# Expert queries in one float32 product instead of three products of parts, and VectorE in GpSimd's place for the residues beside the routing

## The chip, the cores and the metric

The kernel runs on one core of one Trainium2 chip. The metric is the device time of one execution in microseconds (us); the time of a kernel is the median of several executions. The profiler recorded one execution of it, and every row below comes from that record. TensorE is called PE in the rows (PEld its weight loads), VectorE DVE, ScalarE ACT, GpSimd POOL, SyncE SP. Everything is float32 at the level of the model, 256 tokens of width 1024, with 16 more "meta" tokens in the second block.

## The reference, cut to what matters

A first block (two layers of feed-forward, mixed attention, feed-forward) is followed by a second block of two layers. Each of these two layers ends in a "PEER" stage, an expert layer with 16384 experts, and it is the start of that stage that the change touches:

```
def peer(x, wq, subkey1, subkey2, u, v):        # x: normed rows
    q = x @ wq                                  # 8 heads, 2 halves of 128
    s1, s2 = q[half 0] . subkey1, q[half 1] . subkey2    # 128 scores each
    t1, i1 = top_k(s1, 16);  t2, i2 = top_k(s2, 16)
    t, at = top_k(t1[:, None] + t2[None, :], 16)         # 16 experts of a head
    gate = softmax(t)
    # all experts' gelu(x . u_e) * gate_e, summed over v_e
```

In other words: queries, scores, top 16 of each half, the top 16 of their sums, and a softmax over those. That is called the routing here. Beside it the kernel computes gelu(x . u) for all experts densely, and multiplies by the gates afterwards.

## The kernel before, in words

Activations lie transposed: 128 features on the partitions, tokens along the free axis (272 columns in the first PEER stage, 256 in the second, where the meta tokens are dropped).

**Products in three parts.** Most linear layers don't multiply float32 by float32. `weights` (L384) loads a piece of 128x1024 numbers into a tile `w`, and splits each half of it into `wh`, a copy of type float32r made by ScalarE (L398), and `wl`, the residue w - wh (L400), made by VectorE or GpSimd as the letter string `self.lo` says, one letter for each half in turn. Activations are split the same way (`xh`, `xl`, by `split` at L411). `mm3` (L419) then issues three products into one PSUM bank: wh.xh (L422), wh.xl (L423), wl.xh (L424). `w` has a ring of 4 pieces, `wh` and `wl` one of 6 halves each. A few smaller products multiply float32 directly, among them the taps of the conformer's convolution (L1242, 128x128 by 128x272).

**The order of the work** comes from a scheduler that lays the whole program out engine by engine before it runs; each engine then works through its own list strictly in order, and waits where an operand isn't there.

**The rows for the queries.** While the layer before a PEER stage writes its results to `h`, `fresh` (L1175) is called per 128 features; it calls `gained` (L1188), which multiplies h by the norm's gain and splits the product into two tiles of the pair "rr" (ScalarE L1191, VectorE L1192). The division by the root mean square is left for later, since top-k doesn't mind a positive factor.

**The routing** (`route`, L1568): for each of 8 heads, for each half: the weights of the half (L1641), 8 chunks of 128 by `linear` (24 products), a copy of the query (L1645), and two products with the sub-keys (L1649, float32) for two groups of 128 tokens. After both halves `best` (L1591) copies the scores (L1593, ScalarE) and runs VectorE's top-16: MAX (L1562, L1565), index search (L1563, L1566), replacement (L1564), sums (L1600). The 16 meta tokens of all heads go through one more such round at the end. Then `finish` (L1605 to L1635) turns positions into expert numbers and computes the softmax, and `turn` (L1661) transposes the result with three products a group (L1664). Five such groups of L1664 stand on TensorE's list in the first stage (the fifth waits for small DMAs of the meta tokens), four in the second. `keys` (L1483) then casts the result.

**The norm** (`norm`, L1471), called after head 0: the root mean square, eight normed rows (L1475), split into `xh` and `xl`; the residues went to VectorE and GpSimd in turn (`lo="vg"[c % 2]`).

**The experts' first products** (`act`, L1460): for one of 128 groups of 128 experts, one piece of `u`, 24 products with xh and xl, a Gelu. They need nothing of the routing, so that the scheduler lays them beside it. `peer` (L1449) sets `self.lo = "g"` ahead of the routing and for the first 26 of them (PEER_FROM), so that the residues of 16 query pieces and 26 pieces of u, two each, are GpSimd's; from group 26 on it is PEER_LO = 'gv', the two in turn.

Of the kernel before, what the change touches and what calls it, by code (L numbers as in the profile page):

```python
# [17 lines left out]
AF = mybir.ActivationFunctionType  # L18
# [6 lines left out]
T2 = T + NM  # L25
DC = 8
# [3 lines left out]
PIECE, RAW = 1024, 4  # L30
# [155 lines left out]
def _layout1(I):  # L186
# [25 lines left out]
WD = 11  # L212
# [10 lines left out]
W_AN, W_B1, W_DW, W_DB, W_CG, W_CB, W_B2, W_KVN, W_BN, W_FN, W_FIN, W_SUB, W_LAM, NVEC2 = np.cumsum(  # L223
    [0, 8, 16, 8 * CONVW, 8, 8, 8, 8, 8, 8, 16, 8, 1, 4]).tolist()
# [60 lines left out]
class Rows:  # L285
# [6 lines left out]
    z = None  # L292
# [54 lines left out]
class Kernel:  # L347
# [774 lines left out]
    def _second_block(self, ctx, h, out, dump):  # L1122
        nc, I = self.nc, self.I
        self.h = h
        self.rp = self.pool("room", 1, ctx=ctx)
        self.pk = self.pool("pk2", 2, ctx=ctx)
        self.act = self.pool("act2", 1, ctx=ctx)
        nc.scalar.dma_start(h[:, :, 0:NM], I['metaT'])

        def show(n):  # L1130
            if n in dump:
                nc.sync.dma_start(dump[n], h)

        self.following(W_AN, 0, self.pair("xh", "xl"))
        for d in range(DC):
            self.fresh(d, nc.vector if LN_S[d] == 'v' else nc.gpsimd)
        z, s2 = self.z, self.s2
        self.following(W_FN, 0, self.pair("rr"))
        self.conformer(z, s2)
        show('conv')  # L1140
        z, s2 = self.z, self.s2
        self.following(W_KVN, 0, None)
        self.peer(0, 0, z, s2)
        show('peer0')
        z, s2 = self.z, self.s2
        self.following(W_FN + DC, NM, None)
        self.attention(z, s2)
        show('attn')
        z, s2 = self.z, self.s2
        self.following(None, NM, None)  # L1150
        self.peer(1, NM, z, s2)
        r = self.rms_factor(self.s2, NM)[1]
        for c in range(DC):
            nc.vector.scalar_tensor_tensor(h[:, c, NM:], h[:, c, NM:], self.v2(W_FIN + c), r, op0=ALU.mult, op1=ALU.mult)
            if c % 2:
                nc.sync.dma_start(out[:, c - 1:c + 1], h[:, c - 1:c + 1, NM:])
# [5 lines left out]
    def pair(self, *tags):  # L1162
# [3 lines left out]
            return rr[:, 0], rr[:, 1]  # L1166
        return [self.tl(self.act, [128, DC, T2], n, F32R) for n in tags]

    def following(self, gain, t0, parts):

        self.gain, self.t0, self.to = gain, t0, parts
        self.s2 = self.tl(self.act, [128, T2], "ss2", bufs=2)
        self.z = []
# [13 lines left out]

    def gained(self, d, t0, gain, to):  # L1188
        nc, h, g = self.nc, self.h[:, d, t0:], self.v2(gain + d)
        zh, zl = [p[:, d, :T2 - t0] for p in to]  # L1190
        nc.scalar.activation(zh, h, AF.Copy, scale=g)  # L1191
        nc.vector.scalar_tensor_tensor(zl, h, g, zh, op0=ALU.mult, op1=ALU.subtract)  # L1192
        return zh, zl
# [117 lines left out]
    def attention(self, zk, ss):  # L1311
        nc, h, I, C = self.nc, self.h, self.I, self.C2
        mm = nc.tensor.matmul
# [3 lines left out]
        to = self.pair("rr")  # L1317
# [120 lines left out]
                    steps[s](i - lag, n)  # L1438
        self.lo = "v"
        yh, yl = self.pair("xh", "xl")  # L1440
        self.to = self.pair("rr")
        ys = []
        for c in range(DC):
            ys.append((yh[:, c, :T], yl[:, c, :T]))
# [4 lines left out]
    def peer(self, l, t0, z, ss):  # L1449
        nc, h, I = self.nc, self.h, self.I  # L1450
        mm = nc.tensor.matmul
        w = T2 - t0
# [11 lines left out]


        at[0] = ROOM - ROUTE
        self.lo = "g"
        xh, xl = self.pair("xh", "xl")
        x = []

        def norm():  # L1471
            r, ps = self.rms_factor(ss, t0)
            for c in range(DC):
                t = self.tl(self.act, [128, T2], "nrm", bufs=2)[:, :w]
                nc.vector.scalar_tensor_tensor(t, h[:, c, t0:], self.v2(W_FN + DC * l + c), ps, op0=ALU.mult, op1=ALU.mult)  # L1475
                x.append((xh[:, c, :w], xl[:, c, :w]))
                self.split(*x[c], t, lo="vg"[c % 2])
            return r

        self.route(take, ring, l, t0, z, norm, ix)  # L1480
        rr = self.pair("rr")

# [61 lines left out]
        g = 0  # L1544
# [23 lines left out]
    def route(self, take, ring, l, t0, z, norm, ix):  # L1568


        nc, I = self.nc, self.I
        mm = nc.tensor.matmul
        w = T2 - t0
# [17 lines left out]
        def best(r, hd, ps):  # L1591
            s = new_s()
            nc.scalar.activation(s, ps, AF.Copy)  # L1593
            for i in range(2):
                self.top16(r.v[i][:, hd], r.i[i][:, hd], s[:, i])


            c = new_c()
            for o, a, b, n in ((0, 0, 4, 16), (64, 4, 16, 4)):
                nc.vector.tensor_tensor(c[:, o:o + (b - a) * n].rearrange("p (a b) -> p a b", b=n),  # L1600
                                        r.v[0][:, hd, a:b][:, :, None].to_broadcast([128, b - a, n]),
                                        r.v[1][:, hd, 0:n][:, None, :].to_broadcast([128, b - a, n]), op=ALU.add)
            self.top16(r.tv[:, hd], r.tp[:, hd], c)
# [34 lines left out]
        for hd in range(8):  # L1638
            ps = [self.bank("C", 256).rearrange("p (a b) -> p a b", a=2) for _ in chunks]
            for half in range(2):  # L1640
                wq = self.weights(I['f_wq'][l, 2 * hd + half], DC)  # L1641
                pq = self.bank("AD"[half], w)
                self.linear(pq, wq, z)
                q = new_q()
                nc.scalar.activation(q[:, :w], pq, AF.Copy)  # L1645
                if meta:
                    nc.gpsimd.tensor_copy(qm[:, half, hd], q[:, 0:NM])
                for i, c in enumerate(chunks):
                    mm(ps[i][:, half], q[:, c:c + 128], sk[:, half], start=True, stop=True)  # L1649
            if hd == 0:  # L1650
                r = norm()
            for i in range(2):
                best(R[i], hd, ps[i])
# [17 lines left out]
        if meta:  # L1671
            o = take(3, 1, 16)
            finish(M, r[:, 2:3], o)
            t = take(3, 8, 16)
# [40 lines left out]
```

## Time and profile before

| what | value |
|---|---|
| median of 3 executions | 3320.82 us (3313.59 to 3323.24) |
| profiled execution | 3313.82 us, span of its record 3312.0 us |
| first PEER stage: first product with the sub-keys, last L1664 | 1338.5 us, 1478.6 us |
| second PEER stage: the same two | 2430.4 us, 2553.2 us |
| TensorE busy, granted clock in the two stretches | 118.94 of 140.10 us at 0.93; 103.27 of 122.90 us at 0.92 |

The record has 2 us less than the execution that it comes from, and that execution is 7.0 us shorter than the median. Busy time of TensorE counts the pipelined ends of its products, and is longer at a lower granted clock. A window's row gives, for each engine, the busy time in the stretch and the number of instructions.

### The profile page before, as it was taken

The page shows a single profiled execution, that of the slowest core. Times are in us where ns is not written, and L with a number is a line of the kernel's source. Part 1 is how long each engine was busy: PE and PEld are TensorE (multiplying, and loading weights), DVE is VectorE, ACT ScalarE, POOL GpSimd, SP SyncE. Part 2 cuts the span into 40 slices and gives each one's busy share as a digit, 9 for nine tenths or more (in the row PEclk, how much of TensorE's full clock was granted, in tenths as well). Part 3 has the DMA queues.
Part 4 walks back from the last instruction along what each step waited for, and adds up shares of the span by engine and source line. Part 5 has one row for each costly group of instructions (what it writes and reads, how often), then busy time and mean ns, then how long its engine had stood idle before and what let it go on. Part 6 is the DMA issues. An engine that isn't in the chain of part 4 may idle for free.

```text
span 3312.0 us, 69651 instructions
## 1 busy us (share of the span) xinstructions
PE 3182.8 (96%) x27035; PEld 3058.0 (92%) x27035; DVE 2335.8 (71%) x5464; ACT 1663.4 (50%) x3401; POOL 1006.8 (30%) x819
## 2 busy tenths in 40 slices
PE   8999999999999999989999999999998999999998
PEld 8997899999789988889999999999888999999898
DVE  5675676767667578982987549857689397755975
ACT  5564465656546543445444553455354545455454
POOL 0011000001100000764444443444367444444443
PEclk9998899999979999989999999999898999999999
DMA  7652256665215653435444554454244545455454
GB/s 234 188 165 77 75 171 183 185 185 161 80 58 167 184 165 120 134 128 172 148 160 147 165 173 128 157 177 146 89 143 133 185 154 173 153 181 170 135 184 142
DMA packets 140862, 503.14 MB, mean 152 GB/s; under 512 B 17329, under 2 KB 19633, under 8 KB 139889
## 3 DMA queue, kind: packets, MB, share of 16 engines
q1 hardware_dynamic: 137104, 496.06, 47.6%
q8 instruction: 212, 3.47, 0.4%
q10 hardware_dynamic: 3328, 2.36, 0.2%
q14 instruction: 122, 0.99, 0.1%
q0 software_dynamic: 96, 0.26, 0.0%
HBM read 496.36 MB, written 1.05 MB: 150 GB/s over the span
## 4 chain that ended last, share of the span: by engine, by line
PE 75%; DVE 18%; issue 5%; ACT 2%; POOL 0%; DMA 0%; ACTq 0%; SPq 0%; POOLq 0%; DVEq 0%
PE A L422 10%; PE A L423 10%; PE A L424 10%; PE D L422 9%; PE D L423 9%; PE D L424 9%; PE C L422 3%; PE C L423 3%; PE C L424 3%; DVE two L1494 2%; DVE A L1499 2%; DVE wl L400 2%; PE B L758 2%; PE C L1503 1%; DVE room L1600 1%
## 5 line engine op out<-in xcount | busy, mean ns | idle before, releaser
L398 ACT ACTIVATE wh<-w 128x512 fp32r<-128x512 f32 x1856 | 1153.5, 626 | 1284.7 <-PE A L423 507.7
L400 DVE TENSOR_TENSOR wl<-w,wh 128x512 fp32r<-128x512 f32 (+1 forms) x1212 | 859.9, 713 | 550.0 <-ACT wh L398 524.4
L400 POOL TENSOR_TENSOR wl<-w,wh 128x512 fp32r<-128x512 f32 x644 | 888.3, 1385 | 978.1 <-ACT wh L398 938.5
L422 PE MATMUL A<-xh,wh 128*128 128x256 f32 (+2 forms) x1912 | 555.9, 292 | 19.8 <-ACT wh L398 8.4
L423 PE MATMUL A<-xl,wh 128*128 128x256 f32 (+2 forms) x1912 | 554.1, 290 | 3.0 <-DVE xl L330 2.6
L424 PE MATMUL A<-xh,wl 128*128 128x256 f32 (+2 forms) x1912 | 552.3, 289 | 1.3 <-POOL wl L400 1.1
L422 PE MATMUL D<-xh,wh 128*128 128x256 f32 (+2 forms) x1664 | 485.0, 291 | 2.8 <-ACT xh L329 1.5
L423 PE MATMUL D<-xl,wh 128*128 128x256 f32 (+2 forms) x1664 | 480.7, 289 | 3.7 <-DVE xl L330 3.6
L424 PE MATMUL D<-xh,wl 128*128 128x256 f32 (+2 forms) x1664 | 480.1, 289 | 3.8 <-POOL wl L400 3.3
L422 PEld LDWEIGHTS A<-xh,wh 128*128 128x128 f32 x1912 | 368.2, 193 | 24.4 <-ACT wh L398 10.9
L423 PEld LDWEIGHTS A<-xl,wh 128*128 128x128 f32 x1912 | 369.9, 194 | 6.8 <-DVE xl L330 4.9
L424 PEld LDWEIGHTS A<-xh,wl 128*128 128x128 f32 x1912 | 369.8, 193 | 2.8 <-POOL wl L400 1.3
L423 PE MATMUL A<-rr,wh 128*128 128x272 f32 (+1 forms) x1152 | 330.7, 287 | 2.4 <-DVE rr L1192 2.4
L422 PE MATMUL A<-rr,wh 128*128 128x272 f32 (+1 forms) x1152 | 331.2, 288 | 0.8 <-ACT rr L1191 0.8
L424 PE MATMUL A<-rr,wl 128*128 128x272 f32 (+1 forms) x1152 | 329.9, 286 | 0.8 <-POOL wl L400 0.8
L422 PE MATMUL D<-rr,wh 128*128 128x272 f32 (+1 forms) x1152 | 330.3, 287 | 0.0
L424 PE MATMUL D<-rr,wl 128*128 128x272 f32 (+1 forms) x1152 | 329.3, 286 | 0.0
L423 PE MATMUL D<-rr,wh 128*128 128x272 f32 (+1 forms) x1152 | 328.8, 285 | 0.0
L423 PEld LDWEIGHTS D<-xl,wh 128*128 128x128 f32 x1664 | 320.7, 193 | 6.0 <-DVE xl L330 5.8
L422 PEld LDWEIGHTS D<-xh,wh 128*128 128x128 f32 x1664 | 320.3, 192 | 5.8 <-ACT xh L329 3.1
L424 PEld LDWEIGHTS D<-xh,wl 128*128 128x128 f32 x1664 | 320.6, 193 | 5.4 <-POOL wl L400 4.0
L423 PEld LDWEIGHTS A<-rr,wh 128*128 128x128 f32 x1152 | 217.7, 189 | 3.4 <-DVE rr L1192 3.4
(474 smaller groups left out, 6586.7 us busy)
## 6 DMA issues: line engine op xcount, KB each, us to landing
w<-in_u_dram SPq DMA_DIRECT2D x256, 512.0 KB, 3.5
w<-in_v_dram SPq DMA_DIRECT2D x256, 512.0 KB, 3.7
w<-in_ffn_w_dram SPq DMA_DIRECT2D x240, 512.0 KB, 4.4
w<-in_win_f_dram SPq DMA_DIRECT2D x32, 512.0 KB, 3.7
w<-in_f_wq_dram SPq DMA_DIRECT2D x32, 512.0 KB, 3.6
w<-in_ffn_w_dram SPq DMA_DIRECT2D x32, 384.0 KB, 3.1
w<-in_pw_dram SPq DMA_DIRECT2D x24, 512.0 KB, 4.2
w<-in_w_out_dram SPq DMA_DIRECT2D x16, 512.0 KB, 3.8
```

The source lines that it names most:

```text
L398: nc.scalar.activation(h, s, AF.Copy)
L400: (nc.vector if eng == "v" else nc.gpsimd).tensor_tensor(l, s, h, op=ALU.subtract)
L422: mm(ps, wh, xh, start=start, stop=False)
L423: mm(ps, wh, xl, start=False, stop=False)
L424: mm(ps, wl, xh, start=False, stop=stop)
L758: mm(s[:, a:b], q[:, qc * 128:qc * 128 + 128], k[:, :b - a], start=i == 0, stop=False)
L1494: nc.vector.tensor_tensor(two, self.key[:, None].to_broadcast([128, 4, 128, 2]), row(1, 128), op=ALU.is_equal)
L1499: nc.vector.tensor_tensor(A[:, i], one, row(2 + i, n), op=ALU.mult)
L1503: mm(ps[:, k], two[:, k // 2, :, k % 2], A[:, i, k // 2, :, k % 2], start=i == 0, stop=i == 1)
L1600: nc.vector.tensor_tensor(c[:, o:o + (b - a) * n].rearrange("p (a b) -> p a b", b=n), r.v[0][:, hd, a:b][:, :, None].to_broadcast([128, b ...
```

## The change

The queries' products become single float32 products of the raw piece and the raw rows. The tile pair "rr" gives way to one tile of the same bytes (`whole`), `gained` writes the gained rows once, and the route loads each weight piece and multiplies it as it is. Two letters change: `self.lo` ahead of the routing from "g" to "v", which now concerns the 26 pieces of u, and the norm's residues all go to VectorE.

```
@@ second block, and attention's end
-        self.following(W_FN, 0, self.pair("rr"))
+        self.following(W_FN, 0, self.whole())
...
-        self.to = self.pair("rr")
+        self.to = self.whole()
@@
+    def whole(self):
+        return [self.tl(self.act, [128, 2, WD, T2], "rr")[:, 0]]
@@ gained
+        if len(to) == 1:
+            z = to[0][:, d, :T2 - t0]
+            nc.scalar.activation(z, h, AF.Copy, scale=g)
+            return z
         zh, zl = [p[:, d, :T2 - t0] for p in to]
@@ peer
-        self.lo = "g"
+        self.lo = "v"
...
-                self.split(*x[c], t, lo="vg"[c % 2])
+                self.split(*x[c], t)
@@ route
-                wq = self.weights(I['f_wq'][l, 2 * hd + half], DC)
+                wq = self.tl(self.ring, [128, PIECE], "w", bufs=RAW)
+                nc.sync.dma_start(wq, I['f_wq'][l, 2 * hd + half])
                 pq = self.bank("AD"[half], w)
-                self.linear(pq, wq, z)
+                for c in range(DC):
+                    mm(pq, wq[:, c * 128:c * 128 + 128], z[c], start=c == 0, stop=c == DC - 1)
```

The scheduler lays the two PEER starts out anew; on VectorE, ScalarE, GpSimd and SyncE the lists elsewhere are the same. Three places show it. Names end in a number of the tile; line numbers after the change are up to 10 higher (L1649 is L1659, L1624 is L1632, L1626 is L1634, L1627 is L1635).

TensorE in the first routing, a stretch of one head's queries (A and D are PSUM banks of the two halves, C the scores), before:

```order
L1649 MATMUL C_15932<-room_15926 128x128
L1649 MATMUL C_15933<-room_15926 128x128
L422 MATMUL A_16106<-rr_14625,wh_16102 128x272
L423 MATMUL A_16106<-rr_14625,wh_16102 128x272
L424 MATMUL A_16106<-rr_14625,wl_16103 128x272
L422 MATMUL A_16106<-rr_14625,wh_16102 128x272
```

And the same place of a head after:

```order
L1653 MATMUL A_16246<-rr_14625,w_16244 128x272 x5
L1653 MATMUL D_16261<-rr_14625,w_16259 128x272
L1659 MATMUL C_16174<-room_15918 128x128
L1659 MATMUL C_16175<-room_15918 128x128
L1653 MATMUL D_16261<-rr_14625,w_16259 128x272 x7
L1653 MATMUL A_16314<-rr_14625,w_16312 128x272 x3
```

Three entries a chunk have become one, and the products with the sub-keys stand between fewer of them.

GpSimd at the start of the first routing (xl and nrm are the norm's, wl residues of query weights, room_ the queries' meta columns), before:

```order
L1647 COPY room_15926<-room_15926 128x16
L400 TENSOR_TENSOR wl_16331<-w_16328,wh_16330 128x512
L400 TENSOR_TENSOR wl_16335<-w_16328,wh_16334 128x512
L1647 COPY room_15926<-room_15926 128x16
L417 TENSOR_TENSOR xl_15930<-nrm_16030,xh_15929 128x272
L400 TENSOR_TENSOR wl_16370<-w_16367,wh_16369 128x512
```

And after, from the load of the sub-keys to the first residue that GpSimd still has:

```order
L1584 DMA room_15918<-in_sk_dram 128x256
L1657 COPY room_15918<-room_15918 128x16 x2
L435 TENSOR_TENSOR ny_15964<-rv_15962,half_69 128x3
L1657 COPY room_15918<-room_15918 128x16 x14
L400 TENSOR_TENSOR wl_17576<-w_17573,wh_17575 128x512
```

Between the copies nothing is left on GpSimd; its next residue belongs to group 26 of u.

VectorE in the last third of the first routing (`finish`), before:

```order
L1624 TENSOR_TENSOR room_15926<-room_15926,iota_1460_8073 128x1024 x2
L1635 TENSOR_TENSOR room_15926<-room_15926 128x16
L1626 TENSOR_TENSOR room_15926<-room_15926 128x1024
L1617 SCALAR_TENSOR_TENSOR room_15926<-room_15926 128x16
L1626 TENSOR_TENSOR room_15926<-room_15926 128x1024
L1627 TENSOR_REDUCE room_15926<-room_15926 128x64
```

And after:

```order
L1632 TENSOR_TENSOR room_15918<-room_15918,iota_1460_8073 128x1024
L400 TENSOR_TENSOR wl_17466<-w_17463,wh_17465 128x512
L400 TENSOR_TENSOR wl_17470<-w_17463,wh_17469 128x512
L1632 TENSOR_TENSOR room_15918<-room_15918,iota_1460_8073 128x1024
L400 TENSOR_TENSOR wl_17502<-w_17499,wh_17501 128x512
L1634 TENSOR_TENSOR room_15918<-room_15918 128x1024
```

Residues of u stand between the steps of `finish`: 57 of them from the first MAX to the cast in `keys` in the first stage, 55 in the second, where there were none. On TensorE the last group of L1664 stood in the 20th group of u and stands in the 29th.

## Rows read from the trace of the kernel before

**Rows 1.** Page, part 1: busy us (share of the span) and instructions.

```profile
PE 3182.8 (96%) x27035; PEld 3058.0 (92%) x27035; DVE 2335.8 (71%) x5464; ACT 1663.4 (50%) x3401; POOL 1006.8 (30%) x819
```

**Rows 2.** Windows: stretch, length, PE, PEld, DVE, ACT, POOL busy (x), clock, DMA share, GB/s.

```profile
1338.50:1478.60 140.10, 118.94 (x873) 115.55 (x872) 130.38 (x526) 65.32 (x135) 96.71 (x89) 0.93 0.38 119
1478.60:1520.00 41.40, 41.40 (x329) 41.40 (x330) 17.25 (x21) 20.90 (x41) 22.50 (x17) 1.00 0.59 198
...
2430.30:2553.20 122.90, 103.27 (x809) 101.50 (x809) 117.02 (x480) 57.25 (x122) 88.41 (x68) 0.92 0.42 135
2553.20:2600.00 46.80, 46.80 (x398) 46.80 (x398) 23.76 (x22) 25.67 (x50) 30.66 (x23) 1.00 0.59 185
```

**Rows 3.** TensorE's waits, both routings: us, times, longest; last row before the second.

```profile
PE C L1664 <- DVE room L1620: 6.6, 1, 6.6
PE C L1649 <- ACT room L1593: 6.1, 4, 2.0
...
PE C L1664 <- DVE room L1620: 10.5, 1, 10.5
...
PE A L423 <- DVE rr L1192: 2.4, 5, 0.8
```

**Rows 4.** Timeline of DVE and POOL, first routing: start, length, engine, line, operation.

```profile
1345.32 0.20 DVE L1600 TENSOR_TENSOR room<-room 128x48 f32<-128x48 f32 x1
...
1345.70 1.08 DVE L1600 TENSOR_TENSOR room<-room 128x64 f32<-128x64 f32 x1
...
1345.40 1.29 POOL L400 TENSOR_TENSOR wl<-w,wh 128x512 fp32r<-128x512 f32 x1 [0.47 <-ACT wh L398]
```

**Rows 5.** DVE by form, first routing: busy us, mean ns; then 1417.5 to 1423.9.

```profile
L1600 DVE TENSOR_TENSOR room<-room 128x64 f32<-128x64 f32 x17 | 9.5, 559 | 0.0
...
L1626 DVE TENSOR_TENSOR room<-room 128x1024 f16<-128x1024 f16 x8 | 9.5, 1201 | 0.0
...
L1600 DVE TENSOR_TENSOR room<-room 128x48 f32<-128x48 f32 x17 | 9.3, 545 | 0.0
...
L417 DVE TENSOR_TENSOR xl<-nrm,xh 128x272 fp32r<-128x272 f32 x4 | 4.1, 1025 | 0.0
...
L1614 DVE SCALAR_TENSOR_TENSOR room<-room 128x128 f32<-128x128 f32 x2 | 1.6, 812 | 0.0
...
L1600 DVE TENSOR_TENSOR room<-room 128x64 f32<-128x64 f32 x2 | 0.4, 200 | 0.0
...
L1614 DVE SCALAR_TENSOR_TENSOR room<-room 128x128 f32<-128x128 f32 x1 | 0.3, 279 | 0.0
```

**Rows 6.** DVE by form, second routing.

```profile
L1624 DVE TENSOR_TENSOR room<-room,iota 128x1024 f16<-128x1024 f16 x8 | 12.7, 1626 | 0.0
...
L1600 DVE TENSOR_TENSOR room<-room 128x64 f32<-128x64 f32 x16 | 7.7, 480 | 0.0
```

**Rows 7.** Timeline of DVE ahead of the routing; POOL's residues by form, first routing.

```profile
1309.93 1.90 DVE L400 TENSOR_TENSOR wl<-w,wh 128x512 fp32r<-128x512 f32 x3 [0.16 <-ACT wh L398]
...
L400 POOL TENSOR_TENSOR wl<-w,wh 128x512 fp32r<-128x512 f32 x68 | 91.7, 1366 | 45.6 <-ACT wh L398 45.4
```

**Rows 8.** TensorE: L1242 (ns min/median/max); timeline of taps, products with 272, 256 columns.

```profile
L1242 PE MATMUL B<-room x232: 390/392/394, 1214.7 to 1294.7; 128*128 128x272 f32 x116
...
1214.75 5.44 PE L1242 MATMUL B<-room 128*128 128x272 f32 x23
...
1329.31 0.29 PE L422 MATMUL A<-rr,wh 128*128 128x272 f32 x1
...
1331.95 0.28 PE L422 MATMUL D<-rr,wh 128*128 128x272 f32 x1
...
2431.84 0.28 PE L422 MATMUL D<-rr,wh 128*128 128x256 f32 x1
...
2433.97 0.28 PE L422 MATMUL D<-rr,wh 128*128 128x256 f32 x1
```

**Rows 9.** DMA issues, page part 6: KB each, median us to landing.

```profile
w<-in_f_wq_dram SPq DMA_DIRECT2D x32, 512.0 KB, 3.6
```

## The prediction

> **What bounds the kernel now.** I read the page's first part, then windows over the two routings, then TensorE's waits there, then the timeline of VectorE beside GpSimd. Over the whole span TensorE is busy 96% [rows 1], so a change pays where TensorE still loses time. In the two routings it does [rows 2]: from the first product with the sub-keys to the last L1664 it is busy 118.94 of 140.10 us, 21.2 idle, at a granted clock of 0.93 of full speed, which costs 0.07 x 118.9 = 8.3 us; in the second 19.6 idle, and at 0.92 again 8.3. Lost: 29.5 and 27.9 us. Right behind each, TensorE is busy without a gap at clock 1.00 (41.40 of 41.40, 46.80 of 46.80). So what is saved within a routing comes out at the end, unless TensorE itself gets longer.
>
> VectorE is busy 130.4 of 140.1 and 117.0 of 122.9 us [rows 2], and TensorE's longest waits are at L1664 for `finish` and at L1649 for score copies that wait for the top-16 [rows 3]: VectorE bounds both routings. Why is it so slow there? The timeline answers [rows 4]: a sum on L1600 that begins at 1345.32 with GpSimd idle takes 0.20 us; one that begins at 1345.70, after a residue on GpSimd has begun at 1345.40, takes 1.08 and ends as that residue does. GpSimd is busy 96.7 and 88.4 us of the routings [rows 2].
>
> **The change, part by part.**
>
> *TensorE, dearer.* A product of three parts takes three steps. 21 steps lie between 1329.31 and 1331.95, 0.126 each, so 0.377 a product at 272 columns; 18 between 2431.84 and 2433.97, 0.118, so 0.355 at 256 [rows 8]. A float32 product leaves two records; 23 records of the taps take 5.44 us, which without the 0.39 of the last one is 22 steps of 0.23, so 0.46 a product [rows 8]. At 256 columns no such row exists: between 0.43, which is 0.46 x 256/272, and 0.46; I take 0.43. A stage has 8 heads x 2 halves x 8 chunks = 128: 128 x 0.083 = 10.6 us and 128 x 0.078 = 10.0 (13.4 by the upper bound). Nothing hides this once TensorE sets the pace: +20.6.
>
> The Trainium skill, FP8 and Floating Point Precision, TensorE Precision Notes, has true float32 as four passes of the array. Priced as four of this trace's steps, that would be 0.50 a product and +32 instead of +20.6; the taps' row says 0.46, and the row decides.
>
> *VectorE, relieved.* In the first routing 34 sums average 0.552, against 0.20 with GpSimd idle: 34 x 0.36 = 12.2. Four residues of the norm at 1.03 against 0.43: 2.4. In `finish` the 128x128 forms average 0.81 against 0.28 (L1614 is one of them) [rows 5]; the same comparison over its other short forms in that view gives 13.4 in all. Sum 28 us. L1626, eight at 1.20 [rows 5], may give up to 4.8 more, if it is halved as its quicker instances suggest, or nothing; I take nothing. In the second routing: 32 sums x 0.28 = 9.0, L1624 8 x (1.63 - 1.21) = 3.3 [rows 6], the short forms of `finish` 9.7, the norm's residues 1.1: 23.
>
> The Trainium skill, SBUF — State Buffer, Who interferes with whom, calls it an exclusive lock: a VectorE instruction with two SBUF inputs against a GpSimd instruction that reads SBUF, the later one blocked to the other's end. The rows agree (1.08 us, ending with GpSimd's), and by that rule the slow rival below has no ground.
>
> *VectorE, loaded.* From the first MAX to `keys` its list now holds 57 residues of u, 55 in the second stage. Three in a row took 1.90 us, 0.63 each (GpSimd: 1.37) [rows 7]: 36 and 35 us. The norm's four other residues: 4 x 0.36 = 1.4, in the second stage partly ahead of it, about 0.6.
>
> *The balance in the first routing.* VectorE: 130.4 - 28 + 36 + 1.4 = 140 to `keys`; less the 5 us listed behind the fourth L1664 group, plus 2 us from TensorE's first product to VectorE's first MAX: 137 at the fourth group. TensorE up to there: 107 query products x 0.46 = 49.2, 616 steps of u x 0.126 = 77.4, 32 sub-key products 6.9, transposes 3.5: 137. A tie, by lists that give TensorE nine more groups of u before the routing ends than before. In the second: VectorE 117.0 - 23 + 35 + 0.6 = 129.6; TensorE 105 x 0.43 + 624 x 0.118 + 10 = 129. A tie too. In a tie neither engine idles long, but each local lag shows, with the clock behind it. Bounds for what TensorE still loses per routing: 0 (VectorE always ahead by a little) and 20 (the L1649 and L1664 waits stay as they are, about 17 [rows 3], and some clock). Per head, though, TensorE now needs 16 x 0.46 + 0.9 = 8.3 us and VectorE, freed, about 7.5, so the L1649 waits should go; I take 7 each, nearer the lower end.
>
> *Small parts.* In each place where rows are gained, eight residues (L1192) leave VectorE; TensorE waited 2.4 us for them ahead of the second routing [rows 3], -2.4. ScalarE loses 32 copies a stage and was busy 65 of 140 [rows 2]: nothing. GpSimd's release is worth nothing in itself. SyncE issues the same loads in the same order, but a query piece now stays in the ring of 4 until TensorE is done with it, not until it is split. A piece lands 3.6 us after issue [rows 9] and lasts TensorE 8 x 0.46 = 3.7, with three more queued: hidden. The first pieces of u come only as query pieces 13 to 16 go; three pieces, 11 us, cover the 3.6 us and the split. If the cover failed, a few us at this handover. The 57 residues queue behind the top-16 on VectorE, and the products wl.xh wait for them; the 6 halves of the ring are three groups ahead, 9 us.
>
> **Sum.** -29.5 - 27.9 - 2.4 + 10.6 + 10.0 + 7 + 7 = -25. The profiled execution took 3313.8, so 3289 of its kind; it lies 7.0 below the median of the three. Against the median 3320.8 that is 3296, which I predict.
>
> **The rivals.**
> - *VectorE ends the routing after all.* The tie breaks its way (L1626 at full length, residues waiting for ScalarE's copies and passing the delay on to `finish`), and TensorE keeps losing 15 to 20 us a routing: -59.8 + 20.6 + 30 to 40, so 3312 to 3320. For it: lists in strict order, and a margin of 1 to 3 us. Against it: the freed 7.5 us a head against 8.3.
> - *Four steps a float32 product*, 0.50 and 0.47, where the taps' price doesn't carry over to weights fresh from a load: 16 + 15 = 31 in place of 20.6, so 3307. This is the precision page's count. Against it: the taps' 5.44 us.
> - *Slower: the 28 us don't come back.* The place is `finish`. If its long instructions and L1600 stay long for a reason other than GpSimd, VectorE reaches the fourth L1664 group of the first routing at 137 + 28 = 165, TensorE idles 28 there and has 8 of slow clock: 36 in place of 29.5, +10.6; in the second 23 + 8 in place of 27.9, +10.0: +30 - 2.4, about 3349. It decides once less than half comes back: then VectorE ends 11 us or more after TensorE. Against it: 0.20 and 1.08 for one line within half a microsecond [rows 4].
>
> **How the numbers follow.** Another measurement of this kernel can't tell less than 0.3%, 10 us, from no change. Forecast 0.62, all of it faster than 3311. VectorE ending the routing 0.20: 0.04 faster, 0.14 the same, 0.02 slower. Four steps 0.05: 0.03 and 0.02 the same. Slower 0.13: 0.10 slower, 0.03 the same. Faster 0.69, same 0.19, slower 0.12. The forecast's own range is 3277 to 3311: everything lost comes back, -59.8 + 20.6 = -39, counted from the profiled execution, to 16 us left per routing. The range takes in VectorE's case: 3277 to 3322; outside lie the slow rival and a little below.
>
> **What will show it.** L1600's mean near 0.20 in both routings; GpSimd busy under 15 us there; TensorE's waits at L1664 and L1649 (after: L1674, L1659) under 7 us a routing and its clock near 1.00; the query products at 0.46 a pair of records, 0.43 at 256 columns; VectorE's 57 residues at 0.63. Wrong it is if TensorE idles 15 us or more in a routing, if L1600 stays at 0.5, if waits for landing query pieces appear, or if time is lost after the routing, where nothing should change.

## The result, and the profile after

The changed kernel takes 3273.11 us (median of 4 executions, 3270.45 to 3279.23); the kernel before took 3317.2 beside it (3308.28 to 3323.24). The ratio is 0.9877, 95% interval 0.9862 to 0.9892. That is faster, as forecast, but the gain is 44 us where 25 were forecast, and the time lies 4 us below the stated range. The profiled execution of the changed kernel took 3270.45 us, its record 3268.7.

The lines of the changed file stand a little lower: the query product is L1653, the sub-key product L1659 (was L1649), the sum L1608 (L1600), the ix product L1674 (L1664). The first line answers to [rows 1], the windows (columns as in [rows 2], from the first product with the sub-keys to the last ix product, and the stretch behind) to [rows 2]:

```profile
PE 3179.7 (97%) x26779; PEld 3045.3 (93%) x26779; DVE 2311.8 (71%) x5560; ACT 1634.7 (50%) x3339; POOL 777.2 (24%) x643
```

```profile
1336.50:1484.00 147.50, 147.14 (x994) 137.61 (x993) 136.27 (x587) 68.82 (x141) 10.48 (x20) 1.00 0.50 156
1484.00:1530.00 46.00, 46.00 (x365) 46.00 (x366) 16.93 (x27) 23.45 (x46) 19.87 (x16) 1.00 0.61 187
2399.20:2533.00 133.80, 130.68 (x919) 124.69 (x918) 125.26 (x539) 63.65 (x131) 3.88 (x3) 0.99 0.53 166
2533.00:2600.00 67.00, 67.00 (x581) 66.96 (x580) 24.68 (x39) 35.88 (x71) 30.45 (x23) 1.00 0.59 183
```

TensorE idles 0.4 us in the first routing and 3.1 in the second, where it idled 21.2 and 19.6, and its granted clock is 1.00 and 0.99 in place of 0.93 and 0.92. GpSimd is nearly out of the routings. The routings themselves are not shorter: the first took 140.1 us and takes 147.5, the second 122.9 and 133.8. They hold more of TensorE's work. What TensorE still waits for there is next to nothing beside [rows 3]; the first row is the first routing, the others the second:

```profile
PE A L424 <- DVE wl L400: 0.4, 1, 0.4
...
PE D L424 <- DVE wl L400: 1.8, 1, 1.8
PE C L1659 <- ACT room L1601: 1.3, 1, 1.3
```

VectorE by form in the first routing, then two rows of the second (answering to [rows 5, 6, 7]):

```profile
L400 DVE TENSOR_TENSOR wl<-w,wh 128x512 fp32r<-128x512 f32 x57 | 39.7, 700 | 7.3 <-ACT wh L398 7.3
...
L1634 DVE TENSOR_TENSOR room<-room 128x1024 f16<-128x1024 f16 x8 | 5.5, 682 | 0.0
...
L1608 DVE TENSOR_TENSOR room<-room 128x64 f32<-128x64 f32 x17 | 3.5, 207 | 0.0
L417 DVE TENSOR_TENSOR xl<-nrm,xh 128x272 fp32r<-128x272 f32 x8 | 3.4, 431 | 0.0
L1608 DVE TENSOR_TENSOR room<-room 128x48 f32<-128x48 f32 x17 | 3.3, 191 | 0.0
...
L400 DVE TENSOR_TENSOR wl<-w,wh 128x512 fp32r<-128x512 f32 x55 | 36.6, 678 | 6.0 <-ACT wh L398 6.0
L1632 DVE TENSOR_TENSOR room<-room,iota 128x1024 f16<-128x1024 f16 x8 | 9.7, 1218 | 0.0
```

The sums are back at 0.20 us (0.55 before), the norm's residues at 0.43 (1.03), and the multiplication that was L1626 and is L1634 at 0.68 (1.20).

**Where the 43 us lie.** Six instructions that both kernels have (the first tap, the first query copy and the first value sum of each stage, and the lambda scaling that opens the attention) cut each record into stretches. Their lengths in us, for all kernels of this study:

| kernel | to first tap | to query copy | routing 1, to value sum | to attention | attention, to query copy | routing 2, to value sum | rest |
|---|---|---|---|---|---|---|---|
| before | 1214.8 | 121.0 | 363.5 | 543.9 | 184.5 | 338.4 | 545.9 |
| before, again | 1218.9 | 121.0 | 363.5 | 543.9 | 180.8 | 336.5 | 547.8 |
| after | 1210.9 | 121.6 | 343.1 | 544.8 | 174.7 | 325.4 | 548.2 |
| e1 letters | 1217.9 | 122.8 | 338.7 | 543.2 | 184.3 | 319.7 | 549.4 |
| e2 float32 only | 1215.8 | 121.4 | 363.3 | 545.0 | 173.2 | 335.6 | 547.7 |
| e3 first stage | 1213.0 | 121.4 | 342.7 | 544.9 | 182.2 | 338.6 | 548.0 |
| e4 second stage | 1215.9 | 121.8 | 363.6 | 543.9 | 180.5 | 323.7 | 548.2 |
| e6 more VectorE | 1217.8 | 122.2 | 348.0 | 543.5 | 175.7 | 326.0 | 546.9 |
| e7 GpSimd busy | 1221.6 | 121.4 | 348.8 | 545.4 | 171.7 | 333.8 | 548.6 |
| e8 residues kept | 1224.1 | 121.5 | 342.8 | 545.0 | 175.2 | 324.8 | 548.5 |
| e9 memsets | 1216.6 | 121.5 | 342.6 | 542.2 | 173.2 | 323.8 | 549.9 |
| e10 pattern start | 1213.0 | 120.7 | 342.7 | 543.7 | 176.8 | 323.8 | 548.5 |
| c4 | 1215.5 | 121.5 | 341.8 | 538.4 | 173.1 | 322.1 | 538.6 |
| c5 | 1220.4 | 121.4 | 343.0 | 537.9 | 177.4 | 323.6 | 538.8 |
| c6 | 1217.3 | 122.8 | 333.0 | 538.2 | 180.3 | 312.4 | 538.5 |
| c8 | 1217.0 | 123.6 | 333.0 | 538.4 | 176.4 | 311.1 | 539.0 |
| c10 | 1216.5 | 123.5 | 332.9 | 538.4 | 179.4 | 311.1 | 539.1 |

After less before: -3.9, +0.6, -20.4, +0.9, -9.8, -13.0, +2.3, in sum -43.3, the difference of the two records. The first column varies from 1210.9 to 1224.1 us in a part that no kernel changes, so its 3.9 is not the change's. The routings give 33.4, and the end of the attention gives 9.8 that the prediction had at 2.4.

### The profile page after: what moved, and what is told of

Read it like the earlier page. It is cut to its first block, busy times and chain, and to the rows that moved or that the text cites. A ratio compares the mean times of both kernels' runs of the same rounds, so it can differ in the third digit from the quotient of the medians.

```text
span 3268.7 us, 68853 instructions
## 1 busy us (share of the span) xinstructions
PE 3179.7 (97%) x26779; PEld 3045.3 (93%) x26779; DVE 2311.8 (71%) x5560; ACT 1634.7 (50%) x3339; POOL 777.2 (24%) x643
## 4 chain that ended last, share of the span: by engine, by line
PE 81%; DVE 12%; issue 5%; ACT 2%; POOL 0%; DMA 0%; ACTq 0%; POOLq 0%; SPq 0%; DVEq 0%
PE A L422 11%; PE A L423 11%; PE A L424 11%; PE D L422 9%; PE D L424 9%; PE D L423 9%; PE C L422 3%; PE C L423 3%; PE C L424 3%; DVE two L1502 2%; DVE A L1507 2%; DVE wl L400 2%; PE B L758 2%; PE C L1511 1%; PE A L1653 1%
## 5 line engine op out<-in xcount | busy, mean ns | idle before, releaser
L398 ACT ACTIVATE wh<-w 128x512 fp32r<-128x512 f32 x1792 | 1115.4, 626 | 1265.7 <-PE A L423 501.9
L400 DVE TENSOR_TENSOR wl<-w,wh 128x512 fp32r<-128x512 f32 (+2 forms) x1316 | 930.7, 711 | 539.0 <-ACT wh L398 513.8
L400 POOL TENSOR_TENSOR wl<-w,wh 128x512 fp32r<-128x512 f32 x476 | 662.0, 1392 | 1071.0 <-ACT wh L398 1032.7
L424 PE MATMUL A<-rr,wl 128*128 128x272 f32 (+1 forms) x1024 | 293.4, 287 | 0.8 <-POOL wl L400 0.8
L422 PE MATMUL A<-rr,wh 128*128 128x272 f32 (+1 forms) x1024 | 294.0, 287 | 0.0
L422 PE MATMUL D<-rr,wh 128*128 128x272 f32 (+1 forms) x1024 | 293.9, 287 | 0.0
L423 PE MATMUL A<-rr,wh 128*128 128x272 f32 (+1 forms) x1024 | 293.7, 287 | 0.0
L424 PE MATMUL D<-rr,wl 128*128 128x272 f32 (+1 forms) x1024 | 292.7, 286 | 0.0
L423 PE MATMUL D<-rr,wh 128*128 128x272 f32 (+1 forms) x1024 | 292.6, 286 | 0.0
L424 PEld LDWEIGHTS A<-rr,wl 128*128 128x128 f32 x1024 | 194.0, 189 | 1.0 <-POOL wl L400 1.0
```

What stands on the lines that cost most here:

```text
L398: nc.scalar.activation(h, s, AF.Copy)
L400: (nc.vector if eng == "v" else nc.gpsimd).tensor_tensor(l, s, h, op=ALU.subtract)
L422: mm(ps, wh, xh, start=start, stop=False)
L423: mm(ps, wh, xl, start=False, stop=False)
L424: mm(ps, wl, xh, start=False, stop=stop)
```

## The experiments

The theory after the result: GpSimd's residues held VectorE up, and without them TensorE hardly waits; the float32 products only make room on the engines. The rival: the float32 products make the gain. Each kernel's ratio is to the kernel before, timed beside it.

**Which part of the change it was.** e1 changes the letters alone, e2 the products alone:

```
e1 (in before):  self.lo = "g" -> "v" in peer;  self.split(*x[c], t, lo="vg"[c % 2]) -> self.split(*x[c], t)
e2 (in after):   the same two lines put back
```

> The kernel before with the letters alone changed: query products stay in three parts, their 32 weight residues a stage go to VectorE with all others, GpSimd has none in the routings. Theory (GpSimd's residues held VectorE up, and VectorE bounded the routings): sums on L1600 near 0.20 us; VectorE loses 33 us of waiting a routing but takes 89 and 87 residues at 0.70 = 62, so it is some 22 us longer a routing than in the changed kernel, and TensorE idles about 20 a routing in place of 29.5 and 27.9: 3290 to 3312 us. Rival (the float32 products alone make the gain, who makes the residues is nothing): no gain, 3317 or more, with sums still long or VectorE 30 us longer than before.

> The changed kernel with GpSimd again making the residues of the norm's odd rows and of the first keys' weights; query products stay float32. GpSimd then has 57 and 55 residues of u at 1.37 us = 78 us a routing, down from 92. Theory A (both parts are needed: the sums stay at 0.45 to 0.5 us, VectorE bounds the routing again): TensorE idles 8 to 15 us a routing, 3290 to 3305 us. Theory B (float32 products alone are enough: VectorE without the 57 residues but with about two thirds of the held-up time, 130 - 11 = 119 us, is no longer than the 126 it needs in the changed kernel): sums long all the same, TensorE idle under 5 us a routing, 3270 to 3285 us.

e1 takes 3276.54 us, ratio 0.9885 (0.987 to 0.9901): nearly the whole gain, without one float32 query product. e2 takes 3301.53, 0.996 (0.9945 to 0.9974), and by the table none of its gain is in the first routing (363.3) and 2.8 in the second; the rest is the end of the attention. So the letters made the gain of the routings, and the rival is out. The table says more: e1's routing columns are 4.4 and 5.7 us shorter than those of the changed kernel, so there the float32 products cost 10.1 us; at the end of the attention e1 takes 9.6 more, and the two kernels come out level. The first routing of e1 as a window, that of e2 (where TensorE idles 14.5 us), and VectorE by form in that of e1:

```profile
1343.40:1515.00 171.60, 165.13 (x1298) 163.75 (x1296) 162.75 (x617) 93.53 (x186) 29.18 (x30) 0.99 0.46 151
```

```profile
1341.30:1475.00 133.70, 119.16 (x735) 109.31 (x734) 121.60 (x526) 52.23 (x108) 65.99 (x59) 0.95 0.40 127
```

```profile
L400 DVE TENSOR_TENSOR wl<-w,wh 128x512 fp32r<-128x512 f32 x87 | 60.9, 702 | 6.2 <-ACT wh L398 4.5 <-PE C L1649 1.3
...
L1600 DVE TENSOR_TENSOR room<-room 128x64 f32<-128x64 f32 x17 | 3.6, 214 | 0.0
```

But e1 also broke a number of mine. It gives VectorE 87 residues, 30 more than the changed kernel, and I expected TensorE to idle 20 us for it. VectorE's routing did get 24 us longer (171.6 against 147.5), and TensorE idles 6.5. TensorE's list explains it: ahead of the last ix product of the first routing it holds 905 steps of u (688 in the changed kernel, 457 before, 429 in e2). The scheduler knows what a residue on VectorE costs and lays more of u beside it.

**Does TensorE wait for VectorE's load, or for what the lists don't know?** e6 gives VectorE more work that the scheduler counts, e7 holds VectorE up with GpSimd work under routing lists that keep the changed kernel's steps of u, e9 makes GpSimd as busy without reading:

```
e6, in best:   for _ in range(6): nc.vector.max(<8 columns, unused>, s[:, 1])
e7, in route:  for _ in range(6): nc.gpsimd.tensor_tensor(<unused>, q, q, op=ALU.subtract)
e9, in route:  for _ in range(16): nc.gpsimd.memset(<unused>, 0.0)
```

> The changed kernel with six further MAX instructions on VectorE for each of the 17 and 16 top-16 searches of a routing (102 and 96 at 0.28 us: 28 and 27 us of VectorE work, results unused). The scheduler that writes the lists counts them: TensorE's list now has 867 steps of u ahead of the last ix product of the first routing, where the changed kernel has 688 (179 x 0.126 = 22.5 us). Theory (the lists already hold as much TensorE work as VectorE takes; TensorE only waits where VectorE runs later than the list's writer assumed): TensorE idles under 8 us a routing and the time stays within 10 us of the changed kernel, 3270 to 3285 us. Rival (a race between two engines, in which VectorE had 11 us to spare, what it is idle in the changed kernel's first routing): 28 - 11 = 17 and 27 - 13 = 14 us are lost, 3300 to 3308 us.

> The changed kernel with six subtractions on GpSimd for each of the 16 queries of a routing (96 of 128x272 and 128x256, some 0.8 us each: 77 us a routing, results unused, reading only what ScalarE wrote). The lists of VectorE and TensorE in the routings are those of the changed kernel (688 steps of u ahead of the last ix product). Theory (GpSimd's two-input instructions hold VectorE's up, and the lists' writer doesn't know it): sums on L1608's counterpart at 0.4 to 0.6 us, VectorE 20 to 30 us later a routing, TensorE waits at the ix products of 10 to 25 us a routing come back: 3295 to 3325 us. Rival (the gain came from the shorter list of work on TensorE or from the order alone): sums at 0.2, 3268 to 3280 us.

> The changed kernel with 16 memsets on GpSimd for each query (256 a routing, results unused): GpSimd is busy for tens of us in the routing, but reads nothing. Theory (GpSimd's reading is what holds VectorE): L1608's counterpart stays at 0.20 us, time as the changed kernel, 3268 to 3282. Rival (any GpSimd instruction holds a two-input VectorE instruction): its mean at 0.3 us or more, in proportion to GpSimd's busy share.

e6 takes 3279.98 us, 0.9896 (0.988 to 0.9911), 7 above the changed kernel, with intervals that overlap. First routing, its window and its extra instructions:

```profile
1344.10:1519.10 175.00, 171.01 (x1172) 161.56 (x1171) 162.41 (x697) 83.37 (x166) 33.44 (x27) 0.99 0.49 153
```

```profile
L1613 DVE MAX8 more<-room 128x8 f32<-128x128 f32 x102 | 31.8, 368 | 0.0
```

The routing is 27.5 us longer, TensorE idles 4. The records of the extra instructions overlap those behind them: the next instruction starts 0.20 us after one of them, so that they hold VectorE 20.0 us in the first routing and 18.8 in the second, and not the 28 and 27 that I reckoned. A race with 11 and 13 us to spare would still have lost 9 and 6 us; the routing columns lost 4.9 and 0.6. So the race is out, by less than the row suggests.

e7 takes 3289.15 us, 0.9924 (0.9909 to 0.9939): 16 us lost, 5.7 and 8.4 in the routing columns, without a step on TensorE. The sums and GpSimd in the first routing, of e7 and then of e9:

```profile
L1608 DVE TENSOR_TENSOR room<-room 128x64 f32<-128x64 f32 x17 | 6.2, 366 | 0.0
L1608 DVE TENSOR_TENSOR room<-room 128x48 f32<-128x48 f32 x17 | 5.4, 316 | 0.0
...
L1657 POOL TENSOR_TENSOR sq<-room 128x272 f32<-128x272 f32 x92 | 58.7, 671 | 0.0
```

```profile
L1608 DVE TENSOR_TENSOR room<-room 128x64 f32<-128x64 f32 x17 | 4.2, 244 | 0.0
L1608 DVE TENSOR_TENSOR room<-room 128x48 f32<-128x48 f32 x17 | 3.9, 227 | 0.0
...
L1657 POOL MEMSET sq<- 128x272 f32 x238 | 64.3, 316 | 0.0
```

59 us of subtractions on GpSimd make a sum 0.34 us, 64 us of memsets leave it at 0.24. The memsets are also shorter, so the means alone don't separate reading from length; the records one by one do. In the first routing of before all 18 sums that began with GpSimd idle took 0.21 us at most, and the 16 that began in a residue ended 0.06 to 0.08 us after it. In e7 24 of the 26 that began in a subtraction ended about as long after it. In e9 27 began in a memset and took 0.20 to 0.26, eight of them ending before it did, and the six with GpSimd idle took 0.25. Nor does the longer record cost anything there: the next VectorE instruction starts 0.11 us after a sum does in e9, as in the changed kernel (0.26 in e7, 0.47 in before). And e9's time, 3271.66 us (one execution), is that of the changed kernel. The direction is the theory's; the size is not: 16 us lie below the 22 to 52 that I expected. The subtractions are half as long as the residues of before (0.67 against 1.37 us), a sum hit by one waits less, and all 96 (four stand ahead of the row's window) end 19 us before `finish` begins, whose short forms were nearly half of the gain counted for VectorE. The Trainium skill, SBUF — State Buffer, Who interferes with whom, limits the lock for two-input instructions to GpSimd instructions that read SBUF; e7 against e9 agrees.

**Each stage alone, and the end of the attention.**

```
e3 / e4:  float32 product, letter "v" and the norm's split for l == 0 / l == 1 alone, the other stage as before
e8:       gained also computes the residue into an unused tile
e10:      self.nload += 32 ahead of self.lo = ATT_LO
```

> The change in the first stage alone; the second stage as before, the rows ahead of it in two parts. Theory: the first routing gives 20 us (as far as the first gate product came earlier, 23.7, less 3.1 that were there ahead of the routing): 3297 us. If the gain of the changed kernel lies mostly at the end of the attention, where TensorE's list has come in another order and the clock did not fall: 3305 or more.

> The change in the second stage alone, the first as before. Theory: the second routing gives about what it lost, 27.9 less 8 to 10 for the dearer products, and 2.4 for the residues of the rows, so 20 to 22: 3296 us; with the first-stage kernel the gains add up to 44. If the attention's end gives a gain of its own of some 9 us, it belongs to this kernel or to neither: 3288 if to this one.

> The changed kernel with the eight residues of the rows still computed by VectorE in both places (results unused, nobody waits for them). TensorE's list at the end of the attention is the changed kernel's but for a few rows. Theory (the 10 us that the changed kernel gains between the attention and the second routing come from TensorE's list there, in which the clock stays at 1.00, not from the work taken off VectorE): 3268 to 3280 us. Rival (it is the 8 residues, 9 us of VectorE's time ahead of the routing): 3280 to 3290 us.

> The kernel before once more, for a second trace of it. If the 10 us at the end of the attention come from the order of TensorE's list, the stretch from the lambda products to the second routing's first query copy takes 183 to 186 us again and the clock falls to 0.50 there; if the fall of the clock is chance, the stretch may take 172 to 178. The stretch ahead of the convolution varies by some us (1210.9 to 1224.1 us so far), whatever the kernel.

> The changed kernel with the counter of weight pieces put forward by 32 ahead of the attention, to where it stands in the kernel before (a float32 query piece doesn't count its residues, so that the pattern gvv of the attention's letters begins elsewhere). Nothing else differs. Theory (the order at the end of the attention, and with it the fall of the clock there, comes from where the pattern begins): the stretch from the lambda products to the second routing's first query copy takes 180 to 184 us in place of 173 to 176, the time is 3278 to 3285 us. Rival (it comes from the rows' residues alone, which this kernel hasn't): 173 to 176 us, 3270 to 3276.

e3 takes 3290.19 us, 0.9926 (0.9913 to 0.9939), e4 3300.57, 0.996 (0.9947 to 0.9972): 24.7 and 14.3 us, in sum 39 of the 41 that the changed kernel's ratio makes of the before timed beside them. The routing columns agree with the changed kernel's one by one (342.7, 323.7), so the two routings don't help each other.

The end of the attention is another matter. There the clock falls in the kernel before and not in the changed one. Windows: before, before again, after:

```profile
2379.00:2395.00 16.00, 15.67 (x60) 12.78 (x60) 7.44 (x27) 4.76 (x21) 1.85 (x2) 0.50 0.11 33
```

```profile
2379.00:2395.00 16.00, 14.59 (x73) 10.90 (x72) 10.19 (x29) 6.60 (x26) 2.11 (x3) 0.79 0.24 83
```

```profile
2352.00:2368.00 16.00, 15.38 (x104) 12.28 (x103) 13.79 (x42) 8.02 (x29) 3.20 (x4) 1.00 0.31 100
```

In before 60 products in 16 us at 0.50 of full speed (1.2 GHz), in after 104 at 1.00 (2.4 GHz). e8 takes 3273.82 us, 0.9878 (0.9863 to 0.9893): it does the residues and loses nothing, so the VectorE work taken away isn't the gain. What did change is TensorE's list there, and the reason lies far from the diff: `weights` counts its residues in `self.nload`, the attention's letters 'gvv' are picked by that count modulo 3, and a float32 query piece no longer counts its two, 32 in the first stage. e2 and e3, which share this, have the changed kernel's order; e1 and e4 have that of before. But e3 has the order and 182.2 us all the same, and e10, with the start of the pattern put back, showed 176.8 in its record and yet a median of 3280.04 us (3271.48 to 3282.51; 0.9894, 0.9879 to 0.9909), 7 above the changed kernel, with intervals that overlap. By the table, the four records with before's start and before's residues (before twice, e1, c6) have 180.3 to 184.5 us there, the seven with neither to wait for (after, e2, e6 to e9, c4) 171.7 to 175.7, and with one of the two it goes either way: 180.5 (e4), 182.2 (e3), 176.8 (e10), 176.4 (c8). With the letters all "v" (c5, c10) the list has a third order, and the stretch 177.4 us without those residues and 179.4 with them. So both may count, neither alone is shown to be the cause, and how far the clock falls differs between executions of one list. What decides it stays open.

**A kernel faster than both.** If GpSimd's residues cost wherever they meet VectorE, they cost after the routings too.

```
c4 (after) and c6 (e1):  PEER_LO = 'gv' -> 'v'
c5 (c4) and c10 (c6):    the attention's letters all 'v' as well (c5: the convolution's too)
c8 (c6):                 self.nload -= 32 ahead of the attention
```

> The changed kernel with all weight residues of the two expert stages on VectorE, none on GpSimd, the steady part after the routings included (476 residues moved, at 0.65 us 310 us more for VectorE). Theory (GpSimd's residues hold VectorE up beside the gates too: `one` at 0.78 us against 0.35, `two` at 0.89 against 0.68, the split of the gated rows at 0.61 against 0.43): VectorE gets back about 50 us a stage and pays 155, is then busy some 575 of 650 us and still waits for TensorE; of the 25.5 us that TensorE waits for A at the gates up to half go: 3258 to 3275 us. Rival (VectorE becomes the bound in the stretch of gates alone, where it is busy all the time already and would get 37 residues, 24 us, for 13 of relief): 3280 to 3300 us.

> As the last, and the residues of the attention's and of the convolution's weights and rows on VectorE too, so that GpSimd makes no residue behind the first block. Theory: as the last or a few us less where the attention's VectorE work was held up, 3255 to 3275 us. Rival (VectorE's share in the attention rises by a third of its residues, and TensorE waits there): 3280 to 3300 us.

> The kernel with the letters alone (queries in three parts) and, as in the two kernels above, no GpSimd residue in the expert stages. Theory: it stands to the letters-alone kernel (0.9885 of before) as the first of this call stands to the changed kernel (0.988): within 6 us of it. If VectorE becomes the bound, it is the slowest of the three, since it has 64 residues more.

> The kernel with queries in parts and no GpSimd residue in the expert stages (3241 us, stretch 180.3 us), with the counter put back by 32 ahead of the attention, to where it stands in the changed kernel. If the start of the pattern alone decides: stretch 173 to 176, 3233 to 3237 us. If the rows' residues, which this kernel waits for, must be gone as well (the first-stage kernel had this start and the residues, and took 182.2): 180 to 183 us, 3239 to 3245.

> The kernel with queries in parts and no GpSimd residue in the expert stages (3241 us), with the residues of the attention's weights on VectorE too. Theory (GpSimd's residues hold VectorE up wherever the two meet): 3230 to 3241 us. Rival (the attention has no time to give; in the float32 kernels the same step gave 3253.0 and 3254.0): 3238 to 3246 us.

The busy times of c4:

```profile
PE 3176.1 (98%) x26779; PEld 3045.5 (94%) x26779; DVE 2420.3 (74%) x6020; ACT 1633.2 (50%) x3339; POOL 137.2 (4%) x183
```

c4 takes 3253.0 us, 0.9816 (0.9803 to 0.983), better than expected, and 16 of its 17.7 us in the table lie in the two columns behind the value sums; c5 3253.97, so the attention's letters are worth nothing that shows. c6 takes 3241.04, 0.9779 (0.9766 to 0.9793), and I had expected it level with c4. c8 takes 3240.21, 0.9771 (0.9758 to 0.9784), c10 3242.08, 0.9772: neither differs from c6. VectorE in 600 us of the steady part, the changed kernel (1600 to 2200) and c6 (1600 to 2180, its line numbers 8 lower):

```profile
L1502 DVE TENSOR_TENSOR two<-key,sel 128x1024 f16<-128x1024 f16 x85 | 75.4, 887 | 0.0
L417 DVE TENSOR_TENSOR rr<-room,rr 128x272 fp32r<-128x272 f32 x123 | 69.5, 605 | 1.1
L1507 DVE TENSOR_TENSOR A<-one,sel 128x384 f16<-128x384 f16 x102 | 56.5, 593 | 0.0
```

```profile
L1494 DVE TENSOR_TENSOR two<-key,sel 128x1024 f16<-128x1024 f16 x84 | 57.3, 683 | 0.0
L417 DVE TENSOR_TENSOR rr<-room,rr 128x272 fp32r<-128x272 f32 x115 | 44.8, 432 | 0.1
L1499 DVE TENSOR_TENSOR A<-one,sel 128x384 f16<-128x384 f16 x100 | 30.9, 349 | 0.0
```

And c6 has queries in three parts. Between c4 and c6 the routing columns differ by 8.8 and 9.7 us: with GpSimd gone, the float32 products cost nearly what TensorE pays for them and give nothing back there. The medians differ by 12.0 and not by 18.5, since c6's stretch at the end of the attention is 7.2 us longer.

## Why the prediction was right and wrong

*Right: the mechanism.* VectorE bounded the routings, GpSimd's residues held it, and the sums came back to 0.20 us. None of the three rivals came about: the waits at L1664 and L1649 went, and 0.46 a product held against four steps. e7 is the test of the slower rival turned round: bring GpSimd's work back, and the sums grow and the time with them. It brings back 14.1 of the 33.4 us of the routings; that the rest is the same effect, in `finish` and under residues twice as long, is argued and was not tested apart.

*Right: the price of the float32 products.* 14 records at 272 columns and 14 at 256:

```profile
1326.31 3.37 PE L1653 MATMUL A<-rr,w 128*128 128x272 f32 x14
...
2396.09 3.27 PE L1653 MATMUL A<-rr,w 128*128 128x256 f32 x14
2399.20 0.61 PE L1659 MATMUL C<-room 128*128 128x128 f32 x4
```

Without the last one's 0.39, (3.37 - 0.39)/13 = 0.229 a record, 0.458 a product; at 256 columns, with 0.38 for the last, 0.222 and 0.445 where I took 0.43. In all 10.4 + 11.5 = 21.9 us in place of 20.6; c4 against c6 shows 18.5 in the routing columns. (Four steps by the trace's own 0.126 and 0.118 would be 31 us more, as the rival has it, and not 32.)

*Right: VectorE's terms.* A residue's record takes 0.70 and 0.68 us but overlaps the one behind it: until the next instruction starts it holds VectorE 0.62 and 0.60, in all 35.5 and 33.1 us, forecast 36 and 35. Without residues VectorE has 136.3 - 35.5 = 100.8 us in the first routing, against 130.4: 29.6 came back where 28 less 1.4 were counted. L1626, which I had taken as nothing, gave 4.0.

*Wrong: "a tie, I take 7 each".* TensorE lost 0.4 and 3.1 us, and 0.01 x 130.7 = 1.3 by the clock, where 14 were added. That is 9 of the 19 us missed. The error is not the size of the sums but that I raced two engines against each other, over lists that a scheduler had already evened out. e6 and e1 show it: counted work on VectorE, 19 and 20 us more in the first routing, brings more of u into TensorE's list and little waiting. What makes TensorE wait is time that the list's writer didn't count, here the hold-ups by GpSimd.

*Wrong: the end of the attention, 2.4 us.* I priced the wait for L1192 and not the rest of what the trace shows there, 16 us at half clock, and I didn't ask which counters the removed `weights` calls had fed. The record shows 9.8 (6.1 against the second record of before); how much of that a median keeps is open (e10 says 7, c8 against c6 says 1). With 3.9 us ahead of the first tap that are chance, these make up the difference, and they are why the lower end, reckoned as "everything lost in the routings comes back", wasn't low enough. That end was also added up wrongly: -39 from 3313.8 is 3274.6 and not 3277, still above the 3273.1 measured. (16 us left per routing give 3306.6 from there, or 3313.6 from the median, and not 3311.) And of the 23 us between 3296 and 3273.1, 3.6 are no miss of the sum: the median of before moved from 3320.8 to 3317.2 with a fourth execution.

*Not asked: whether both parts of the change were needed.* The sum added them up; e1 shows that the letters do all of the routings' gain and more (24.8 + 18.7 us of its columns, against 20.4 + 13.0), and that the float32 products are a loss there (10.1 us beside e1, 18.5 between c4 and c6).

## What to carry to other kernels

Price a two-input GpSimd instruction by what it does to VectorE's two-input instructions beside it: here 460 residues more on VectorE (x643 to x183 on GpSimd), some 285 us of work at 0.62 each, raised its busy time by 108 us (2311.8 to 2420.3) and made the kernel 20 us faster (c4 against after). Where a scheduler writes the lists, work that it counts moves the other engines' work along; look for time that it doesn't count. And when a change drops a call, look for the counters that the call fed, since a pattern far away may start elsewhere.

## What the runs showed of the hardware that was not expected

Memsets keep GpSimd as busy as subtractions and take nothing from VectorE: a sum's record is a little longer beside them (0.24 us), but the next instruction starts as early as without (0.11 us after it). The f16 instructions of the gates are held too: the product A takes 0.35 us alone and 0.59 beside GpSimd's residues. Of instructions with one input (lines of before), the scaling L1634 of 128x8 was held in its first routing (1.24 us, 0.17 in the changed kernel), the reduction L1627 was not (1.20 and 1.21). In e6 the record of a MAX of 128x128 is 0.37 us long, where it is 0.28 in the changed kernel, and yet the next instruction starts 0.19 to 0.20 us after it in both; why the records are longer was not tried. What a VectorE instruction costs is read from the start of the next one, not from its record.
